# Batched 64 x 64 matmul: the first loads of b behind the first load of a, and the last casting loads one store later

## The chip, the cores and the metric

The kernel runs on one core of a Trainium2 chip. Its engines, each with its own instruction stream, are PE (matmul and weight load), DVE (vector), ACT (scalar), POOL (GpSimd) and SP (which only issues transfers here). Sixteen DMA engines move data between the HBM and the core's on-chip memory. The metric is the device time of one execution in microseconds, the median of several runs. One further execution is taken by the hardware profiler; all traces are from such executions.

## The reference

```python
def setup_inputs():
    return {
        "a": np.random.randn(1024, 64, 64).astype(np.float32),
        "b": np.random.randn(1024, 64, 64).astype(np.float32),
    }

def reference(a: np.ndarray, b: np.ndarray) -> np.ndarray:
    return np.matmul(a, b).astype(np.float32)
```

There are 1024 independent products of 64 x 64 matrices. Each of a, b and the output is 16.78 MB in float32.

## The kernel before

**Tiles.** a is worked in 8 tiles s of 128 batches, b and the output in 16 tiles t of 64 batches (`n_s` = 8, `n_t` = 16). A tile of a is 2.1 MB in HBM and becomes bf16 on its way in; a tile of b or of the output is 1.05 MB in float32.

**Loads of a** (`load_a`, L61 to L68). Four transfers per tile, one for each h, each writing 256 KB of bf16. They are issued by POOL[...]. Three buffers (`A_AHEAD` = 3).

**Loads of b** (`load_b`, L70 to L74). One transfer of 1.05 MB per tile, float32, issued on ACT for tiles 1 and 3 and on SP for the others. Four buffers (`B_AHEAD` = 4); a buffer comes free when `cast` (L111, on ACT) has made a bf16 copy of it.

**The last tile of b is different** (L112 to L115). Tile 15 isn't loaded in float32. `cast(15)` issues four transfers on POOL that write bf16 straight into `b_bf`, four rows of groups each. They wait for that buffer, which the product of tile 13 reads last.

**Compute.** `regroup(s)` (L79, DVE) reorders a tile of a; `transpose(s, w)` transposes it on PE (L88) with an identity matrix, and DVE (L94) and ACT (L96) copy the results out of PSUM; `spread(t)` (L106, DVE) lays half a tile out in blocks of 32 columns; `multiply(t)` runs 64 matmuls (L144) in four quarters, and each quarter is copied to `o_sb` by ACT (L156; in the last tile, every second quarter by DVE, L154).

**Stores** are issued by POOL, one output tile in one transfer of 1.05 MB (`put_all`, L134), the last tile in four of a quarter each (`put`, L128). A store is called one tile late (`HOLD` = 2): iteration t of the main loop issues the store of tile t - 1. There are five output buffers.

**Order.** All instructions stand in the order in which the code is written (`tc.manual_schedule()`), and each engine works its own instructions in that order. POOL's instructions, in order: the four loads of a's tile 0, a memset and an affine select that build the identity (in the helper `make_identity`), eight loads of a's tiles 1 and 2; then further loads of a mixed with the stores; at the end the stores of tiles 11 and 12, the four casting loads of tile 15, the stores of tiles 13 and 14, and the four quarter stores of tile 15. POOL's transfers form one queue. An issue on POOL also waits for the landing of the one eight places before it, since there are eight semaphores for them. SP starts with b's tiles 0 and 2, ACT with 1 and 3; neither waits for anything before its first issue but the program's start.

```python
        load_a(0)
        for t in range(B_AHEAD):
            load_b(t)
        for bd in bd_tiles:
            nc.vector.memset(bd[:], 0.0)
        make_identity(nc, identity)
        for s in range(1, A_AHEAD):
            load_a(s)
```

Of the kernel before, what the change touches and what calls it, by code (L numbers as in the profile page):

```python
# [7 lines left out]

fp32 = mybir.dt.float32
# [4 lines left out]
def kernel(  # L14
# [13 lines left out]
    nc = tc.nc  # L28
# [4 lines left out]
    n_t, n_s = B // 64, B // 128  # L33
# [6 lines left out]
    b_v = b.rearrange("(t g h) (kp u) n -> t (h kp) g (u n)", h=4, g=16, u=2)  # L40
# [16 lines left out]
    ]  # L57
    identity = consts.tile([128, 128], bf16)
    a_tiles, b_tiles, abf_tiles, at_tiles, bbf_tiles = {}, {}, {}, {}, {}
    held = {}  # L60

    def load_a(s):
        a_sb = a_pool.tile([128, 4, 16, 64], bf16, name="a_sb")
        for h in range(4):
            nc.gpsimd.dma_start(  # L65
                out=a_sb[:, h, :, :].rearrange("p v k -> p (v k)"), in_=a_v[s, h]
            )
        a_tiles[s] = a_sb  # L68

    def load_b(t):  # L70
        b_sb = b_pool.tile([128, 16, 128], fp32, name="b_sb")
        queue = nc.scalar if t in (1, 3) else nc.sync
        queue.dma_start(out=b_sb[:], in_=b_v[t])  # L73
        b_tiles[t] = b_sb  # L74

    def regroup(s):
        a_sb = a_tiles.pop(s)
        a_bf = work.tile([128, 16, 4, 64], bf16, name="a_bf")
        nc.vector.tensor_copy(a_bf[:], a_sb[:].rearrange("p h v k -> p v h k"))  # L79
        abf_tiles[s] = a_bf  # L80
        at_tiles[s] = work.tile([128, 2, 2, 128, 8], bf16, name="at_sb")

    def transpose(s, w):
        a_cols = abf_tiles[s][:].rearrange("p v h k -> p v (h k)")
        for u in range(2):
            at_ps = t_psum.tile([128, 8, 128], bf16, name="at_ps")
            for vo in range(8):
                nc.tensor.transpose(  # L88
                    at_ps[:, vo, :], a_cols[:, 2 * vo + w, u::2], identity[:]
                )  # L90
            dst = at_tiles[s][:, w, u, :, :]
            src = at_ps[:].rearrange("p vo q -> p q vo")
            if u == 0:
                nc.vector.tensor_copy(dst, src)  # L94
            else:
                nc.scalar.copy(dst, src)  # L96

    def spread(t):
        at_v = at_tiles[t // 2][:].rearrange(
            "p w u (g mp) vo -> p (w u) g (mp vo)", g=32  # L100
        )
        half = slice(16 * (t % 2), 16 * (t % 2) + 16)
        bd_v = bd_tiles[t % N_BD][:].rearrange("p (wu g) h mo -> p wu g h mo", g=16)
        for h in range(4):
            rows = slice(32 * h, 32 * h + 32)
            nc.vector.tensor_copy(bd_v[rows, :, :, h, :], at_v[rows, :, half, :])  # L106

    def cast(t):
        b_bf = work.tile([128, 16, 128], bf16, name="b_bf")
        if t < n_t - 1:  # L110
            nc.scalar.copy(b_bf[:], b_tiles.pop(t)[:])  # L111
        else:  # L112
            for gq in range(4):
                rows = slice(4 * gq, 4 * gq + 4)
                nc.gpsimd.dma_start(out=b_bf[:, rows, :], in_=b_v[t, :, rows, :])  # L115
        bbf_tiles[t] = b_bf

    def store(t):
        for piece in held.pop(t):
            piece()  # L120

    def multiply(t):
        at_bd, b_bf = bd_tiles[t % N_BD], bbf_tiles.pop(t)
        last = t == n_t - 1
        o_sb = o_pool.tile([128, 4, 4, 2, 64], fp32, name="o_sb")

        def put(gq):
            nc.gpsimd.dma_start(  # L128
                out=o_v[t, :, 4 * gq : 4 * gq + 4, :],
                in_=o_sb[:, gq, :, :, :].rearrange("p g w n -> p (g w n)"),  # L130
            )

        def put_all():
            nc.gpsimd.dma_start(  # L134
                out=o_v[t], in_=o_sb[:].rearrange("p q g w n -> p (q g w n)")
            )

        for gq in range(4):
            o_ps = o_psum.tile([128, 4, 2, 64], fp32, name="o_ps")
            for g4 in range(4):  # L140
                g = 4 * gq + g4
                for w in range(2):
                    for u in range(2):
                        nc.tensor.matmul(  # L144
                            o_ps[:, g4, w, :],
                            at_bd[:, (2 * w + u) * 16 + g, :, :].rearrange(
                                "p h mo -> p (h mo)"
                            ),
                            b_bf[:, g, 64 * u : 64 * u + 64],
                            start=(u == 0),  # L150
                            stop=(u == 1),
                        )
            if last and gq % 2:
                nc.vector.tensor_copy(o_sb[:, gq, :, :, :], o_ps[:])  # L154
            else:
                nc.scalar.copy(o_sb[:, gq, :, :, :], o_ps[:])  # L156
        held[t] = [lambda q=q: put(q) for q in range(4)] if last else [put_all]

    with tc.manual_schedule():
        load_a(0)  # L160
        for t in range(B_AHEAD):
            load_b(t)
        for bd in bd_tiles:
            nc.vector.memset(bd[:], 0.0)  # L164
        make_identity(nc, identity)
        for s in range(1, A_AHEAD):
            load_a(s)
        regroup(0)
        transpose(0, 0)
        transpose(0, 1)  # L170
        spread(0)
        cast(0)
        regroup(1)
        load_a(A_AHEAD)
        transpose(1, 0)
        for t in range(n_t):
            s, half = t // 2, t % 2
            if t + 1 < n_t:
                spread(t + 1)
            if half == 0:  # L180
                if s + 2 < n_s:
                    regroup(s + 2)
                if s + 1 + A_AHEAD < n_s:
                    load_a(s + 1 + A_AHEAD)
            multiply(t)
            if t + 1 < n_t:
                cast(t + 1)
            if t + B_AHEAD < n_t - 1:
                load_b(t + B_AHEAD)
            if half == 0 and s + 1 < n_s:  # L190
                transpose(s + 1, 1)
            if half == 1 and s + 2 < n_s:
                transpose(s + 2, 0)
            if t >= HOLD - 1:
                store(t - HOLD + 1)
        for t in range(n_t - HOLD + 1, n_t):
            store(t)

# [29 lines left out]
```

## Time and profile before

| what | value |
|---|---|
| median of 3 runs | 138.66 us (138.46 to 138.76) |
| the profiled execution | 139.03 us |
| its span, first to last instruction | 137.2 us |
| busy: PE, PEld, DVE, ACT, POOL | 59.1, 56.9, 84.5, 76.6, 45.6 us |
| HBM read, written | 33.55 MB, 16.78 MB |
| POOL's queue (a, casting loads, stores) | 25.69 MB as written, 69.9% of 16 engines' span |
| SP's and ACT's queues (b) | 13.63 and 2.10 MB, 28.4% and 4.1% |

The span is 1.8 us shorter than the execution's own time. The busy shares are averages over the whole span. A DMA share is the busy time of 16 engines; packets of different queues can overlap on one engine, so that a share in a short stretch may come out over 1. The GB/s of the profile count bytes as they are written, so a load that casts from float32 to bf16 counts with half of what it reads. "Landing" is the last semaphore update of a transfer. Times within the span are counted from the first instruction.

### The profile page before, as it was taken

The numbers are of one execution on the slowest core, as the hardware profiler recorded it, in microseconds if no ns is written. First come the engines' busy times: TensorE is split into PE (matmuls) and PEld (weight loads), VectorE is DVE, ScalarE is ACT, GpSimd is POOL, SyncE is SP. The second block draws the span as 40 slices with busy tenths as digits, with TensorE's granted clock in tenths as the row PEclk, the third lists the DMA queues.
The fourth block names the chain that finished last, engine by engine and source line by source line (L and its number), as shares of the span: only waits on it lengthen the run. The fifth ranks groups of instructions, "written<-read, shape, count | busy, mean of one in ns | idle before, by whom it ended". The sixth has DMA issues, their size and how long they took to land.

```text
span 137.2 us, 2992 instructions
## 1 busy us (share of the span) xinstructions
PE 59.1 (43%) x1280; PEld 56.9 (42%) x1280; DVE 84.5 (62%) x92; ACT 76.6 (56%) x96; POOL 45.6 (33%) x61
## 2 busy tenths in 40 slices
PE   0000072295764586450397206980085633095300
PEld 0000071295774486450396206880085633094200
DVE  5770168789799999998179903995059819501200
ACT  1030018059999999905976078840979694553100
POOL 6811242344145503351132833300213114804700
PEclk9999999559999999999559955599559995559555
DMA  2999999999999999999999999999999999999991
GB/s 72 291 304 310 303 282 260 209 256 269 237 262 274 382 295 270 318 376 374 287 269 340 377 365 274 270 364 375 382 384 379 382 382 380 382 216 315 337 289 41
DMA packets 19053, 41.61 MB, mean 303 GB/s; under 512 B 3168, under 2 KB 3168, under 8 KB 19040
## 3 DMA queue, kind: packets, MB, share of 16 engines
q0 software_dynamic: 11120, 25.69, 69.9%
q1 hardware_dynamic: 6864, 13.63, 28.4%
q10 hardware_dynamic: 1056, 2.10, 4.1%
q8 instruction: 10, 0.16, 0.5%
q14 instruction: 3, 0.02, 0.0%
HBM read 33.55 MB, written 16.78 MB: 367 GB/s over the span
## 4 chain that ended last, share of the span: by engine, by line
DMA 27%; SPq 22%; ACT 19%; issue 10%; POOL 7%; PE 6%; DVE 3%; POOLq 1%; DVEq 0%; ACTq 0%
SPq L73 22%; DMA b_sb<-in_b_dram 17%; DMA a_sb<-in_a_dram 10%; ACT o_sb L156 8%; ACT b_bf L111 6%; ACT at_sb L96 5%; PE at_ps L88 4%; POOL b_bf L115 2%; PE o_ps L144 2%; DVE a_bf L79 2%; POOL out_dram L134 2%; POOL out_dram L128 2%; DVE at_bd L106 1%; POOL a_sb L65 1%; POOLq L223 1%
## 5 line engine op out<-in xcount | busy, mean ns | idle before, releaser
L144 PE MATMUL o_ps<-b_bf,at_bd 128*128 128x64 bf16 x1024 | 41.1, 209 | 45.6 <-ACT b_bf L111 43.9
L144 PEld LDWEIGHTS <-at_bd 128*128 128x128 bf16 x1024 | 40.2, 109 | 47.5 <-issue 37.1
L106 DVE COPY at_bd<-at_sb 32x2048 bf16<-32x2048 bf16 x64 | 46.8, 731 | 21.3 <-ACT at_sb L96 20.3
L156 ACT COPY o_sb<-o_ps 128x512 f32<-128x512 f32 x62 | 33.9, 622 | 24.2 <-DMA out_dram<-o_sb 16.2
L65 POOL DMA_DIRECT2D a_sb<-in_a_dram x32 | 19.6, 617 | 39.0 <-DMA a_sb<-in_a_dram 27.2
L134 POOL DMA_DIRECT2D out_dram<-o_sb x15 | 19.2, 1278 | 38.7 <-ACT o_sb L156 21.7
L111 ACT CAST b_bf<-b_sb 128x2048 bf16<-128x2048 f32 x15 | 29.2, 1945 | 4.2 <-DMA b_sb<-in_b_dram 4.2
L88 PE MATMUL at_ps<-identity,a_bf 128*128 128x128 bf16 x256 | 20.4, 245 | 23.4 <-DVE a_bf L79 23.4
L88 PEld LDWEIGHTS <-a_bf 128*128 128x128 bf16 x256 | 18.0, 112 | 23.6 <-DVE a_bf L79 23.6
L96 ACT COPY at_sb<-at_ps 128x1024 bf16<-128x1024 bf16 x16 | 16.9, 1056 | 16.8 <-PE at_ps L88 16.8
L94 DVE COPY at_sb<-at_ps 128x1024 bf16<-128x1024 bf16 x16 | 19.5, 1222 | 4.2 <-PE at_ps L88 4.1
L79 DVE COPY a_bf<-a_sb 128x4096 bf16<-128x4096 bf16 x8 | 10.4, 1303 | 7.6 <-DMA a_sb<-in_a_dram 7.4
L164 DVE MEMSET at_bd<- 128x4096 uint32 x2 | 6.9, 3472 | 2.5 <-PEq L212 1.7
L154 DVE COPY o_sb<-o_ps 128x512 f32<-128x512 f32 x2 | 1.4, 692 | 8.8 <-PE o_ps L144 8.8
L115 POOL DMA_DIRECT2D b_bf<-in_b_dram x4 | 3.2, 806 | 4.8 <-ACT o_sb L156 4.8
L96 ACT ACT_TABLE_LOAD x1 | 1.3, 1283 | 4.4 <-issue 4.4
L128 POOL DMA_DIRECT2D out_dram<-o_sb x4 | 3.0, 754 | 1.6 <-ACT o_sb L156 0.9
L73 ACT MOVE_SHAPE b_sb<-in_b_dram x2 | 0.6, 320 | 1.7 <-issue 0.9
masks.py:199 POOL TENSOR_SCALAR_AFFINE_SELECT identity<-identity 128x128 bf16<-128x128 bf16 x1 | 0.3, 287 | 0.1
masks.py:197 POOL MEMSET identity<- 128x128 bf16 x1 | 0.3, 271 | 0.0
L212 POOL MEMSET const-float32-0.0<- 128x1 f32 x1 | 0.1, 98 | 0.2 <-issue 0.2
L212 POOL MEMSET const-bfloat16-1.0<- 128x1 bf16 x1 | 0.1, 101 | 0.0
(2 smaller groups left out, 0.2 us busy)
## 6 DMA issues: line engine op xcount, KB each, us to landing
out_dram<-o_sb POOLq DMA_DIRECT2D x15, 1024.0 KB, 21.2
a_sb<-in_a_dram POOLq DMA_DIRECT2D x32, 256.0 KB, 16.4
out_dram<-o_sb POOLq DMA_DIRECT2D x4, 256.0 KB, 7.1
b_bf<-in_b_dram POOLq DMA_DIRECT2D x4, 128.0 KB, 9.7
b_sb<-in_b_dram SPq DMA_DIRECT2D x13, 0.5 KB, 22.4
b_sb<-in_b_dram ACTq DMA_DIRECT2D x2, 0.5 KB, 18.4
```

Source lines behind the costliest of these rows:

```text
L65: nc.gpsimd.dma_start(out=a_sb[:, h, :, :].rearrange("p v k -> p (v k)"), in_=a_v[s, h])
L73: queue.dma_start(out=b_sb[:], in_=b_v[t])
L79: nc.vector.tensor_copy(a_bf[:], a_sb[:].rearrange("p h v k -> p v h k"))
L88: nc.tensor.transpose(at_ps[:, vo, :], a_cols[:, 2 * vo + w, u::2], identity[:])
L94: nc.vector.tensor_copy(dst, src)
L96: nc.scalar.copy(dst, src)
L106: nc.vector.tensor_copy(bd_v[rows, :, :, h, :], at_v[rows, :, half, :])
L111: nc.scalar.copy(b_bf[:], b_tiles.pop(t)[:])
L134: nc.gpsimd.dma_start(out=o_v[t], in_=o_sb[:].rearrange("p q g w n -> p (q g w n)"))
L144: nc.tensor.matmul(o_ps[:, g4, w, :], at_bd[:, (2 * w + u) * 16 + g, :, :].rearrange("p h mo -> p (h mo)"), b_bf[:, g, 64 * u : 64 * u + 6 ...
L156: nc.scalar.copy(o_sb[:, gq, :, :, :], o_ps[:])
L164: nc.vector.memset(bd[:], 0.0)
```

## The change

Two places are edited, and the imported helper that built the identity is written out.

First, the memset of the identity tile moves to POOL's stream between the first and the second load of a's tile 0, and the loads of b's tiles 0 (on SP) and 1 (on ACT) get a dependence on that memset. As an engine works in order, the memset comes after POOL has issued the first load of a. The affine select stays where it was, behind the four loads of tile 0.

Second, in the iteration t = 14 of the main loop, `cast(15)` comes after `store(13)` instead of ahead of it. POOL's order at the end becomes: stores of tiles 11, 12 and 13, the four casting loads, the store of tile 14, the four quarter stores. No other engine's order changes.

```diff
@@ -57,11 +56,13 @@
-    held = {}
+    held, begun = {}, []
 
     def load_a(s):
         a_sb = a_pool.tile([128, 4, 16, 64], bf16, name="a_sb")
         for h in range(4):
+            if s == 0 and h == 1:
+                begun.append(nc.gpsimd.memset(identity[:], 0.0))
             nc.gpsimd.dma_start(
                 out=a_sb[:, h, :, :].rearrange("p v k -> p (v k)"), in_=a_v[s, h]
             )
@@ -70,7 +71,16 @@
         queue = nc.scalar if t in (1, 3) else nc.sync
-        queue.dma_start(out=b_sb[:], in_=b_v[t])
+        load = queue.dma_start(out=b_sb[:], in_=b_v[t])
+        if t < 2:
+            tc.add_manual_dep(
+                load.ins,
+                begun[0].ins.name,
+                mybir.DependencyInfo(
+                    mybir.DependencyClass.Sync, mybir.DependencyReason.DATA
+                ),
+                reason="first load of a goes ahead",
+            )
         b_tiles[t] = b_sb
@@ -162,7 +172,15 @@
-        make_identity(nc, identity)
+        nc.gpsimd.affine_select(
+            out=identity[:],
+            in_=identity[:],
+            compare_op=mybir.AluOpType.not_equal,
+            fill=1.0,
+            base=0,
+            pattern=[[-1, 128]],
+            channel_multiplier=1,
+        )
@@ -183,7 +201,7 @@
             multiply(t)
-            if t + 1 < n_t:
+            if t + 1 < n_t - 1:
                 cast(t + 1)
@@ -193,6 +211,8 @@
             if t >= HOLD - 1:
                 store(t - HOLD + 1)
+            if t == n_t - 2:
+                cast(t + 1)
```

More of the change, by code (lines that the diff above doesn't have):

```diff
@@ L5 @@
 from concourse import bass_utils, mybir
-from concourse.masks import make_identity
 from concourse._compat import with_exitstack
```

## The prediction

> **What bounds the kernel now.** I read the 40 slices first, then the queues and landings, then the chain of waits, then the stretches at both ends, because the change touches the first 4 us and the last 23 us.
>
> ```profile
> DMA  2999999999999999999999999999999999999991
> DMA packets 19053, 41.61 MB, mean 303 GB/s; under 512 B 3168, under 2 KB 3168, under 8 KB 19040
> ...
> SPq L73 22%; DMA b_sb<-in_b_dram 17%; DMA a_sb<-in_a_dram 10%; ACT o_sb L156 8%; ACT b_bf L111 6%; ACT at_sb L96 5%; PE at_ps L88 4%; POOL b_bf L115 2%; PE o_ps L144 2%; DVE a_bf L79 2%; POOL out_dram L134 2%; POOL out_dram L128 2%; DVE at_bd L106 1%; POOL a_sb L65 1%; POOLq L223 1%
> ```
>
> The DMA row is the bound: 38 of 40 slices show the 16 engines busy for 90% or more, while DVE, the busiest compute engine, has 62%. The chain of waits names a's first tile, ACT work and then SP's queue. I give that chain less weight: it follows who released whom, but if the engines always have other bytes to move, a wait that goes only changes the order of the bytes. The time is then first byte, plus bytes at the rate their mix allows, plus the drain.
>
> The stretches at the start, in time order (columns: length, busy time of PE, PEld, DVE, ACT, POOL, clock, DMA share, GB/s counted as written):
>
> ```profile
> 1.00:2.00 1.00, 0.00 (x0) 0.00 (x0) 0.33 (x1) 0.32 (x1) 0.71 (x2) 1.00 0.00 0
> 2.00:3.00 1.00, 0.00 (x0) 0.00 (x0) 1.00 (x1) 0.30 (x1) 1.00 (x2) 1.00 0.52 139
> 3.00:4.00 1.00, 0.00 (x0) 0.00 (x0) 1.00 (x1) 0.00 (x0) 0.93 (x4) 1.00 0.90 215
> 4.00:5.00 1.00, 0.00 (x0) 0.00 (x0) 1.00 (x1) 0.00 (x0) 1.00 (x3) 1.00 1.01 352
> 5.00:6.00 1.00, 0.00 (x0) 0.00 (x0) 0.20 (x2) 0.00 (x0) 1.00 (x3) 1.00 1.08 291
> ```
>
> The first bytes move after 2 us and the rate climbs for 2 us. The timeline says whose they can be:
>
> ```profile
> 0.79 0.86 ACTq L73 DMA_DIRECT2D b_sb<-in_b_dram  x1
> 0.80 24.16 SPq L73 DMA_DIRECT2D b_sb<-in_b_dram  x3
> 1.29 2.32 POOL L65 DMA_DIRECT2D a_sb<-in_a_dram  x4 [0.84 <-POOLq L212]
> ...
> 16.77 1.23 DVE L79 COPY a_bf<-a_sb 128x4096 bf16<-128x4096 bf16 x1 [7.36 <-DMA a_sb<-in_a_dram]
> ```
>
> b's loads are issued 0.5 us ahead of a's. In the packet records b0 has its first packet at 2.39 us, a0 its first at 4.93 and b1, issued on ACT at 0.79, at 5.18: SP's load has the engines alone for 2.5 us. From there on a and b share, and a0 is complete at 16.65.
>
> The end:
>
> ```profile
> 114.97 3.20 POOL L115 DMA_DIRECT2D b_bf<-in_b_dram  x4 [4.77 <-ACT o_sb L156]
> 118.16 1.27 POOL L134 DMA_DIRECT2D out_dram<-o_sb  x1
> 124.32 1.16 POOL L134 DMA_DIRECT2D out_dram<-o_sb  x1 [4.89 <-ACT o_sb L156]
> 124.82 3.30 PE L144 MATMUL o_ps<-b_bf,at_bd 128*128 128x64 bf16 x64 [1.42 <-DMA b_bf<-in_b_dram]
> 129.39 0.75 POOL L128 DMA_DIRECT2D out_dram<-o_sb  x1 [0.55 <-DVE o_sb L154]
> ...
> 118.00:120.00 2.00, 0.15 (x4) 0.15 (x4) 0.66 (x1) 1.79 (x1) 1.43 (x2) 0.50 1.03 385
> 122.00:124.00 2.00, 1.40 (x27) 1.26 (x24) 0.00 (x0) 1.48 (x3) 0.00 (x0) 0.69 1.60 184
> 128.00:130.00 2.00, 0.12 (x3) 0.00 (x0) 0.69 (x1) 0.00 (x0) 1.36 (x2) 0.50 1.02 326
> 131.00:132.00 1.00, 0.00 (x0) 0.00 (x0) 0.00 (x0) 0.00 (x0) 0.00 (x0) 0.50 1.02 291
> 134.00:135.00 1.00, 0.00 (x0) 0.00 (x0) 0.00 (x0) 0.00 (x0) 0.00 (x0) 0.50 0.22 86
> ```
>
> POOL's queue works in order: stores 11 and 12, the four casting loads of tile 15, store 13, store 14, four quarter stores of tile 15. The casting loads land at 124.69, 125.53, 126.32 and 127.04, store 13 at 129.82, store 14 at 132.72, the quarters at 133.66 to 135.77. The last quarter is issued 2.35 us after the last casting load lands (129.39 - 127.04) and lands 6.38 us after its issue, because it stands behind a backlog. Stores alone run at 385 GB/s at 118 us and at 291 at 131 us; the casting loads fill the engines at only 184 (122 to 124).
>
> **What the Trainium skill says.** "DMA: Bandwidth & Descriptors", section "Queues, rings and completion order": each engine round-robins between its queues, a packet at a time. From 5 us on the trace agrees (a and b share); in the first 2.5 us it doesn't, since b1 and a0 had been issued and got nothing.[...] The same page, "Latency and other measured facts", gives about 0.6 us to the first byte for a load from SP or ACT and about 1 us for one from GpSimd. Here SP's took 1.59 us (0.80 to 2.39), longer; GpSimd's alone on idle engines is in no part of this trace. "Anatomy of one DMA" says that most of some 2 us fixed cost is the wait for the write's receipt; the trace has 0.43 us from the last packet's end (135.34) to the last landing (135.77).
>
> **The change part by part.**
>
> Part 1, the start. The memset moves between a0's first and second issue. POOL's first issue ends at 1.98; with 0.27 for the memset (its own row) the marker is set at about 2.25, and the first b loads on SP and ACT go at about 2.3 instead of 0.8, so 1.5 us later. Behind them on the same queues stand b2 (SP, at 2.06 before), b3 (ACT, at 2.33, its issue lasting 4.32 us) and ACT's table load at 6.68. All shift by some 1.5 us. b2 and b3 would land by about 20 and 25.5 and are cast after 36; the table is first used at 19.98: covered. a0's other three issues shift by 0.27 us, but chunk 0 keeps the queue busy for longer; the affine select is wanted by the first transpose only. The explicit memset and select replace the helper's same two instructions: nothing.
>
> What isn't covered is the engines' idle time. From the windows, before moved 139 + 215 + 352 + 291 = 997 KB as written by 6.0 us; 83 KB of that are a's, by the packet records, and each is two bytes read, which makes about 1,080 KB of HBM traffic. With the gate, b's first packet is at about 2.3 + 1.59 = 3.9, and a's is unknown: not before 1.98 + 0.6 = 2.6, not after 4.93 as now. At the early end a alone at about 400 GB/s (a and b together carry 400 to 404 from 6 us on) moves 1,360 KB by 6.0, a gain of 280 KB or 0.7 us. At the late end, b alone from 3.9 with before's climb (some 510 KB in its first 2.1 us) and a as now (166 KB) move some 680 KB, a loss of 1.0 us. I take the middle, about 3.5 us: 2.5 us at an average of 395 give 990 KB, a loss of 90 KB, **+0.2 us**.
>
> a0 comes earlier: with up to 2.5 us of the engines to itself it may land near 12 to 14 instead of 16.65. Compute and b4's load (which waits for the first cast, now 22.3 to 24.2) then start earlier too. I cost that at nothing: between 18.2 and 28.3 SP's queue is without a packet, but a's own chunks keep the engines full. What is late next is the DMA engines.
>
> Part 2, the end. Store 13 goes ahead of the casting loads. It waits for the copies of tile 13 (done at 115.02), so it issues at about 115.1 (1.27 us), and the loads at 116.3 to 119.5 instead of 114.97 to 118.17: covered, as the queue reaches them after 120 only. Nobody else waits behind POOL until store 14 at 124.3. In the queue a store of 256 packets at 174 ns over 16 engines takes 2.8 us, so the casting loads land 2.8 us later, the last at 129.8, and the last quarter issues at 132.2 instead of 129.4. The bytes after that are unchanged. Whether this costs depends on the least time from issue to landing: 0.75 for the issue, 0.6 to 2.5 for the first packet, 0.8 for four packets per engine at about 200 ns, 0.43 to the landing, so 2.6 to 4.5 us. It then lands at 134.8 to 136.7 where the backlog allows 135.77: 0 to +0.9; I take 3.8 us, so 136.0: **+0.25 us**. Below zero: with store 13 moved away, the final run of stores is 2 MB instead of 3 MB. If the slow 291 GB/s comes from that run's length, 1.05 MB at 385 instead of 291 saves 0.9 us, capped at 0.7 by the latency.
>
> Sum: 139.03 (span 137.2 and 1.83 around it) + 0.2 + 0.25 = 139.48 on the profiled execution; that one was 0.37 above the median, so **139.1** for the median. A difference of 0.2% is 0.28 us, about what a measurement here can tell.
>
> **Rivals.**
> - Start gains. a's stream reaches idle engines before 3.0 us and runs at full rate at once, where b climbed slowly: -0.5 at the start (from 2.8 us at 400 GB/s: 1,280 KB against 1,080), tail hidden: 138.66 - 0.5, 138.1 to 138.2. For: from 2.39 to 4.0 us b moved 354 KB, where 400 GB/s would give 640. Against: cold first packets could slow a in the same way. It decides from a first a packet at about 3.0 us on downwards.
> - Tail gains. The write run after the casting loads is shorter and faster, -0.7, with +0.2 at the start: 138.2. For: 385 against 291 GB/s. Against: the 2 MB moved ahead may become slow instead.
> - All hidden. The same bytes, the same full engines, a0 and b0 swap places: 138.7.
> - Both exposed. a doesn't start before 4.5 us (+1.0), and the last quarter has the long latency (+0.7): 140.3. For: today's 4.93.
> - The change doing nothing at the start (b issued late but a not ahead) falls under the last.
>
> **How the numbers follow.** Forecast 0.38, start gains 0.18, tail gains 0.18, all hidden 0.14, both exposed 0.12. The forecast's own range is 138.9 to 139.7, and a little of it (0.02) lies within 0.2%. Faster 0.36, same 0.16, slower 0.48. The range 137.8 to 140.3 takes in both gains with 0.3 us to spare and reaches to the exposed case.
>
> **What would show it.** A first a packet at 2.6 to 4 us and DMA GB/s near 0 from 2 to 3; a0's regroup on DVE well before 16.77; the first cast on ACT earlier, though the end doesn't follow. At the end store 13 issued ahead of the casting loads, these landing 2 to 3 us later, a last quarter issued near 132 and landing in 4 us or less, and DMA share below 1 before it. I am wrong if the span falls by over 0.3 us, in particular if the earlier compute carries through to the end: then the DMA engines weren't the bound that I read.

## The result, and the profile after

The changed kernel takes 142.71 us, median of six runs (141.57 to 143.48), against 138.51 us (138.29 to 138.76) for the kernel before: a ratio of 1.0293, 95% interval 1.0233 to 1.0353. A second set of six runs gave 141.96 us against 138.53, ratio 1.0246 (1.0215 to 1.0277). It is slower by 3.4 to 4.2 us, where 0.45 us was forecast. The profiled execution took 141.57 us, 2.54 us more than the one before (139.03); the fastest run of its set was profiled, so the traces show less of the loss than the medians.

The page of the changed kernel: the span, the DMA and GB/s rows of the 40 slices, and the shares of the chain of waits.

```profile
span 139.8 us, 2992 instructions
...
DMA  2999999999999999999999999999999999999973
GB/s 19 189 307 306 305 307 304 298 271 250 230 273 268 373 304 269 318 372 375 284 271 342 381 355 274 274 373 379 383 383 372 387 382 382 318 260 155 287 217 109
...
DMA 56%; issue 27%; POOL 13%; POOLq 1%
DMA a_sb<-in_a_dram 38%; DMA out_dram<-o_sb 17%; POOL out_dram L144 6%; POOL a_sb L66 3%; POOL b_bf L125 2%; POOL out_dram L138 2%; POOLq L243 1%; POOL identity L175 0%; POOL identity L65 0%; POOLq L144 0%; POOLq L175 0%; POOLq L138 0%; POOLq L125 0%; POOLq L66 0%; POOLq L232 0%
```

In the first two slices 19 and 189 GB/s stand where 72 and 291 stood, but these count bytes as written, and up to 6.4 us all of them are a's, of which twice as many are read. The last six slices have 318, 260, 155, 287, 217 and 109. SP's queue, 22% of the chain before, is gone from it: the chain now runs along POOL's own queue (a's loads 38%, the stores 17%).

The stretches at the start (columns: length; busy time of PE, PEld, DVE, ACT, POOL; clock; DMA share; GB/s as written), and one instruction of the timeline:

```profile
2.00:3.00 1.00, 0.00 (x0) 0.00 (x0) 1.00 (x1) 0.02 (x1) 1.00 (x3) 1.00 0.49 33
3.00:4.00 1.00, 0.00 (x0) 0.00 (x0) 1.00 (x1) 0.62 (x1) 0.95 (x3) 1.00 0.77 86
4.00:5.00 1.00, 0.00 (x0) 0.00 (x0) 1.00 (x1) 0.00 (x0) 1.00 (x3) 1.00 1.09 201
5.00:6.00 1.00, 0.00 (x0) 0.00 (x0) 0.20 (x2) 0.00 (x0) 1.00 (x3) 1.00 1.12 199
```

```profile
12.97 1.23 DVE L89 COPY a_bf<-a_sb 128x4096 bf16<-128x4096 bf16 x1 [3.56 <-DMA a_sb<-in_a_dram]
```

a goes ahead as it was meant to: its first packet is at 2.66 us (4.93 before), and tile 0 is regrouped at 12.97 instead of 16.77. b's tile 0, issued at 2.28, has its first packet at 6.44: now b waits behind a, as a did behind b. By 6.0 us the engines have moved 33 + 86 + 201 + 199 = 519 KB as written, 1,038 KB read. In the profile of before they have moved 1,098 KB (the prediction counted 83 KB of a's there; its packet records have 49 packets of 2,048 B, 100 KB). That profile is the lowest of six runs with the old opening, which have 1,098 to 1,264 KB, 1,186 in the mean; the four runs with both gates have 1,036 to 1,075, 1,052 in the mean. At 400 GB/s the start costs 0.15 us in bytes by the two profiles and 0.3 us by the means.

The end, as timeline (start, length, engine, line, operation) and as stretches:

```profile
115.49 1.23 POOL L144 DMA_DIRECT2D out_dram<-o_sb  x1 [3.42 <-ACT o_sb L166]
...
116.70 3.20 POOL L125 DMA_DIRECT2D b_bf<-in_b_dram  x4
...
130.36 3.57 PE L154 MATMUL o_ps<-b_bf,at_bd 128*128 128x64 bf16 x64 [8.39 <-DMA b_bf<-in_b_dram]
...
134.95 0.75 POOL L138 DMA_DIRECT2D out_dram<-o_sb  x1 [0.21 <-issue]
```

```profile
118.00:120.00 2.00, 1.36 (x31) 1.36 (x31) 1.57 (x2) 1.15 (x2) 1.90 (x3) 0.74 1.04 365
122.00:124.00 2.00, 0.00 (x0) 0.00 (x0) 0.00 (x0) 0.59 (x1) 1.11 (x1) 0.91 1.01 287
126.00:128.00 2.00, 0.00 (x0) 0.00 (x0) 0.00 (x0) 0.00 (x0) 0.00 (x0) 0.50 1.24 134
132.00:134.00 2.00, 1.93 (x37) 1.77 (x34) 0.72 (x2) 0.59 (x1) 1.53 (x3) 0.50 0.50 170
136.00:138.00 2.00, 0.00 (x0) 0.00 (x0) 0.00 (x0) 0.00 (x0) 0.00 (x0) 0.50 0.78 229
```

PE sits idle for 8.39 us before the last tile, waiting for a casting load (1.42 before). The casting loads land at 130.22 to 132.43 instead of 124.69 to 127.04, 5.4 us later, and the last quarter store is issued at 134.95 and lands at 138.39, 3.44 us after its issue: there is no backlog ahead of it any more. From 132 to 134 the DMA share is 0.50: on average half of the engines have no work while the last product is made. Stores alone fall from 365 to 287 GB/s between 118 and 124. From 124 on the casting loads are in the count, with half of what they read: 134 GB/s from 126 to 128, against 184 in the like stretch before (122 to 124).

One more reading of the traces carries what follows. The Trainium skill, "DMA: Bandwidth & Descriptors", section "Why a DMA increments its semaphore by 16 and not by 1", says that each of the 16 engines adds one to a transfer's semaphore when its own share has landed. The traces agree: POOL's transfers have 16 updates each. The time between the first and the last of them is how far the engines are out of step, called the spread here. For the fourth and last chunk of a's tile 0 it is 0.53 us before and 2.16 us after. It doesn't stay at that: by the store of tile 9, at about 112 us, the two kernels have 2.31 and 3.11 us. With 16 updates, the ninth stands here for the middle engine.

### The profile page after: what moved, and what is told of

Same layout as the page of the kernel before. It is cut to its first block, busy times and chain, and to the rows that moved or that the text cites. A ratio compares the mean times of both kernels' runs of the same rounds, so it can differ in the third digit from the quotient of the medians.

```text
span 139.8 us, 2992 instructions
## 1 busy us (share of the span) xinstructions
PE 62.0 (44%) x1280; PEld 59.7 (43%) x1280; DVE 85.3 (61%) x92; ACT 77.1 (55%) x96; POOL 46.4 (33%) x61
## 3 DMA queue, kind: packets, MB, share of 16 engines
q1 hardware_dynamic: 6864, 13.63, 27.6%
## 4 chain that ended last, share of the span: by engine, by line
DMA 56%; issue 27%; POOL 13%; POOLq 1%
DMA a_sb<-in_a_dram 38%; DMA out_dram<-o_sb 17%; POOL out_dram L144 6%; POOL a_sb L66 3%; POOL b_bf L125 2%; POOL out_dram L138 2%; POOLq L243 1%; POOL identity L175 0%; POOL identity L65 0%; POOLq L144 0%; POOLq L175 0%; POOLq L138 0%; POOLq L125 0%; POOLq L66 0%; POOLq L232 0%
## 5 line engine op out<-in xcount | busy, mean ns | idle before, releaser
L154 PE MATMUL o_ps<-b_bf,at_bd 128*128 128x64 bf16 x1024 | 42.5, 213 | 50.3 <-ACT b_bf L121 36.4
L154 PEld LDWEIGHTS <-at_bd 128*128 128x128 bf16 x1024 | 41.7, 112 | 52.1 <-issue 41.0
L116 DVE COPY at_bd<-at_sb 32x2048 bf16<-32x2048 bf16 x64 | 47.6, 744 | 19.6 <-ACT at_sb L106 18.6
L66 POOL DMA_DIRECT2D a_sb<-in_a_dram x32 | 20.1, 641 | 39.9 <-DMA a_sb<-in_a_dram 29.2
L98 PE MATMUL at_ps<-identity,a_bf 128*128 128x128 bf16 x256 | 21.9, 255 | 21.7 <-DVE a_bf L89 21.7
L98 PEld LDWEIGHTS <-a_bf 128*128 128x128 bf16 x256 | 19.3, 118 | 22.0 <-DVE a_bf L89 22.0
```

The source lines that it names most:

```text
L66: nc.gpsimd.dma_start(out=a_sb[:, h, :, :].rearrange("p v k -> p (v k)"), in_=a_v[s, h])
L98: nc.tensor.transpose(at_ps[:, vo, :], a_cols[:, 2 * vo + w, u::2], identity[:])
L154: nc.tensor.matmul(o_ps[:, g4, w, :], at_bd[:, (2 * w + u) * 16 + g, :, :].rearrange("p h mo -> p (h mo)"), b_bf[:, g, 64 * u : 64 * u + 6 ...
```

## The experiments

Ratios are to the kernel before in the same batch (medians of 138.24 to 138.56 us), with 95% intervals. Spreads and landings, in us, are from each run's one profile.

| run | median us | ratio (95%) | spread, a's 4th chunk | spread, store of tile 9 | last casting load | last landing |
|---|---|---|---|---|---|---|
| before | 138.51 | | 0.53 | 2.31 | 127.04 | 135.77 |
| after | 142.71 | 1.0293 (1.0233 to 1.0353) | 2.16 | 3.11 | 132.43 | 138.39 |
| after_again | 141.96 | 1.0246 (1.0215 to 1.0277) | 2.15 | 3.12 | 133.16 | 139.13 |
| gate_only | 140.91 | 1.0175 (1.0149 to 1.0201) | 3.07 | 4.62 | 128.15 | 137.76 |
| cast_only | 139.34 | 1.0059 (1.0038 to 1.0080) | 0.67 | 2.85 | 130.55 | 136.33 |
| gate_b0 | 138.98 | 1.0030 (1.0017 to 1.0044) | 1.02 | 2.46 | 127.75 | 136.00 |
| gate_b1 | 138.95 | 1.0022 (1.0008 to 1.0037) | 1.10 | 2.72 | 127.58 | 135.84 |
| late_all | 139.74 | 1.0073 (1.0044 to 1.0101) | 0.70 | 2.70 | 128.35 | 136.73 |
| after_reads | 144.20 | 1.0422 (1.0402 to 1.0443) | 1.90 | 3.42 | 135.45 | 141.22 |
| deep_b | 144.91 | 1.0465 (1.0440 to 1.0489) | 0.99 | 4.11 | 133.36 | 141.60 |
| b3 | 141.27 | 1.0202 (1.0165 to 1.0238) | 0.57 | 1.84 | 126.69 | 138.27 |
| store13_sp | 139.27 | 1.0070 (1.0058 to 1.0083) | 0.65 | 2.66 | 130.42 | 135.96 |
| store1314_sp | 139.49 | 1.0091 (1.0077 to 1.0106) | 0.77 | 2.73 | 131.19 | 136.21 |

### Each half alone

`gate_only` is the changed kernel with the old order at the end:

```diff
-            if t + 1 < n_t - 1:
+            if t + 1 < n_t:
                 cast(t + 1)
...
-            if t == n_t - 2:
-                cast(t + 1)
```

> Only the first half of the change: the gate on the first two b loads, the casting loads ahead of store 13 as before. Theory S (the prediction's start term was right, the loss is all at the end): +0.1 to +0.4 us on the median of before, so 138.6 to 138.9. Theory R (the earlier end of b's loads, 116.6 against 117.8, is what lengthens the run of pure stores and slows the end): +1 us or more.

`cast_only` is the kernel before with the new order at the end, that is, with these lines the other way round.

> Only the second half: store 13 ahead of the casting loads, no gate. Theory S: the whole loss but 0.2 us is here, so +2.4 to +4.5 us, 141 to 143, with the last casting load landing 4 us or more later than the 127.04 of before and under 4 us from the last quarter's issue to its landing. Theory R: under +2 us, since b ends at its old time.

The gate alone costs 1.75% (2.4 us), the casting loads' place 0.59% (0.8 us). Theory S is refuted: most of the loss is in the half that it priced at 0.2 us. The two add up to 2.34%, within the intervals of both measurements of the whole change (2.33 to 3.53 and 2.15 to 2.77). Theory R, which put the loss on b's earlier end, was right on both numbers, but this doesn't make its mechanism the cause: in gate_only b ends at 117.10, only 0.72 us before the 117.82 of before, and gate_b1, below, ends b earlier still (116.87) and costs 0.3 us.

The end of before, and then of gate_only, in the same columns (the line of before from 134 to 135 us has a share of 0.22):

```profile
133.00:134.00 1.00, 0.00 (x0) 0.00 (x0) 0.00 (x0) 0.00 (x0) 0.00 (x0) 0.50 0.73 250
...
135.00:136.00 1.00, 0.00 (x0) 0.00 (x0) 0.00 (x0) 0.00 (x0) 0.00 (x0) 0.50 0.01 4
```

```profile
133.00:134.00 1.00, 0.00 (x0) 0.00 (x0) 0.00 (x0) 0.00 (x0) 0.00 (x0) 0.50 0.90 279
134.00:135.00 1.00, 0.00 (x0) 0.00 (x0) 0.00 (x0) 0.00 (x0) 0.00 (x0) 0.50 0.38 148
135.00:136.00 1.00, 0.00 (x0) 0.00 (x0) 0.00 (x0) 0.00 (x0) 0.00 (x0) 0.50 0.12 45
136.00:137.00 1.00, 0.00 (x0) 0.00 (x0) 0.00 (x0) 0.00 (x0) 0.00 (x0) 0.50 0.07 25
```

A DMA share of 0.07 is one engine of sixteen (0.0625). From 136 us on a single engine works off its part of the last stores, with 15 done. In the last store's 16 updates the ninth comes at 134.65 (134.53 before) and the last at 137.76 (135.77 before). The middle engine is 0.12 us later than before, the last one 1.99 us. As a pool the engines lost almost nothing; one of them is late, and the kernel waits for it.

That this is the lag of the start, carried along, the trace doesn't show. The engines of before get out of step too, only later: their spread is 0.5 us up to 28 us, 1.7 at 35.6, and 2.2 to 2.5 from 41 to 113 us. In gate_only it falls from 3.1 to 2.1 us by 37 us, rises to 4.9 at 46, and is 4.6 for store 9. At store 12 (last update 124.02) the last engine is only 1.25 us behind the middle one, where before has 1.44. The straggler of the end comes up after that: from the last casting load to store 13 the last update takes 4.41 us (128.15 to 132.56) and the ninth 2.74 (125.72 to 128.46). In that stretch the packet records have one packet of the queue that the page calls q8 instruction, 16 KB from 130.48 to 131.51. before has one as well (128.58 to 129.61), without such a step. Whether the slowest engine served it isn't shown, so this packet stays an untested rival for a part of the 1.99 us.

In cast_only the engines stay in step at the start (0.67 us) and the end is the one that the prediction described, a little larger:

```profile
122.00:124.00 2.00, 0.82 (x19) 0.70 (x16) 0.00 (x0) 1.17 (x2) 0.25 (x1) 0.87 1.05 278
...
130.00:132.00 2.00, 2.00 (x38) 1.84 (x35) 0.69 (x1) 0.66 (x2) 1.45 (x2) 0.50 0.56 196
```

Stores alone slow to 278 GB/s ahead of the casting loads, and while the last product is made (130 to 132) the share is 0.56. The last casting load lands at 130.55, 3.51 us later than before. The last quarter store follows it by 2.48 us (issue at 133.03) and lands 3.30 us after that.

### Which part of the gate costs

`gate_b0` and `gate_b1` gate one of the two loads only (`if t == 0:` and `if t == 1:` in place of `if t < 2:`; base: gate_only). `late_all` keeps both gates but puts b ahead of a again, everything later:

```diff
-            if s == 0 and h == 1:
-                begun.append(nc.gpsimd.memset(identity[:], 0.0))
+            if s == 0 and h == 0:
+                for i in range(6):
+                    begun.append(nc.gpsimd.memset(identity[:], 0.0))
...
-                begun[0].ins.name,
+                begun[3].ins.name,
```

> The gate on b's tile 0 (SP) alone; tile 1 on ACT is free, the end as before. Theory J (the cost of the gate is that a long stream of b joins DMA engines that a already keeps busy, which puts the 16 engines out of step and leaves one of them to finish last): b's tile 1 now runs ahead of a, a joins it, so the four landings of a's tile 0 stay within 1 us between first and last engine for most chunks, and the time is 138.3 to 139.3. Theory G (it costs what it costs because SP's first load is late): as with the whole gate, 140.5 or more.

> The gate on b's tile 1 (ACT) alone; tile 0 on SP is free, the end as before. Theories J and G: no cost, 138.1 to 138.7, since tile 1 had no packet before 5.18 us anyway. Theory P (any late join of a queue costs, also ACT's): 139 or more.

> Six memsets on POOL ahead of a's first load, b's first two loads gated on the fourth of them: all first loads are about 1.5 us later and b is ahead of a as in the kernel before. Theory J: the engines stay in step (landings of a's tile 0 within 0.8 us between the engines) and the time grows by the shift alone, +1.2 to +1.7 us, with the last engine finishing 1 to 1.5 us after the middle one as before. Theory G (waiting on POOL for the first b loads is itself what puts the engines out of step): +3 us or more.

gate_b0 costs 0.30%, gate_b1 0.22%, both gates together 1.75%. So neither load's lateness is the cost: while one b load still runs ahead of a, the other can be late for 0.3 to 0.4 us. Theory G is refuted by gate_b0, and in its other form by late_all. gate_b1 came out above its expected range, by a little, so a late second queue isn't quite free (spread 1.10 against 0.53).

late_all has both gates too, and holds b's loads until 1.82 us (gate_only 2.29) and a's first until 2.19 (1.30), yet it costs 0.73% (1.0 us), less than gate_only and a little less than expected. Its first b packet is at 3.41 us, 1.0 us later than before, and a's at 4.96, the old order, and the spread is 0.70. Its end:

```profile
134.00:135.00 1.00, 0.00 (x0) 0.00 (x0) 0.00 (x0) 0.00 (x0) 0.00 (x0) 0.50 0.69 242
135.00:136.00 1.00, 0.00 (x0) 0.00 (x0) 0.00 (x0) 0.00 (x0) 0.00 (x0) 0.50 0.19 74
136.00:137.00 1.00, 0.00 (x0) 0.00 (x0) 0.00 (x0) 0.00 (x0) 0.00 (x0) 0.50 0.01 4
```

The drain has the shape of before, 1 us later (0.73, 0.22, 0.01 from 133 on there). The middle engine ends at 135.27 and the last at 136.73: a shift of the whole, no straggler. All four runs with both gates have a spread of 1.90 to 3.07 us in a's fourth chunk; the nine in which a load of b runs ahead of a have 0.53 to 1.10. So it is the order, a alone on the engines when both b queues come in, that puts the engines out of step in the first 14 us, and the same order costs 2.4 us where a single late load costs 0.3 or 0.4 and the late start in the old order 1.0. Why an engine falls back in that order isn't shown: the records don't say which engine a packet ran on. In gate_only the spread is 0.63 us for a's first chunk, 1.41 for the second, and 3.07 for the fourth, that is, it grows between 5 and 14 us, while b's queues (first packets 5.83 and 6.91) come in.

### Stores without loads beside them

`stores_only` leaves everything out but 16 full stores from five tiles of zeros. `after_reads` adds two loads of b behind tile 14's, to tiles that nobody reads:

```diff
                 load_b(t + B_AHEAD)
+                if t + B_AHEAD == n_t - 2:
+                    for i in range(2):
+                        more = consts.tile([128, 16, 128], fp32, name=f"more{i}")
+                        nc.sync.dma_start(out=more[:], in_=b_v[i])
```

> Leaves out all loads and all arithmetic: five tiles of zeros are stored to the 16 output tiles on the same queue. Theory W (a run of stores without loads beside it slows down after about 3 us): about 380 GB/s in the first 3 us of traffic, 260 to 310 afterwards, the 16.78 MB in about 55 to 60 us. Theory E (the slow rate belongs to the end of this program, to the mix of queued transfers or to the tile's work beside it): 370 to 385 GB/s throughout, about 44 us.

> The changed kernel with two more loads on SP behind b's tile 14, 2.1 MB of b read again into tiles that nobody uses; the output is unaffected. Theory W: while these reads run, from about 116 to 130 us, all traffic together is near 380 GB/s where the changed kernel had 300 or less from 119.5 to 125, so the added bytes (5.5 us at 380 GB/s) cost 3 us at most. Theory E: the rate stays near 300 or less in that stretch and the time grows by 5 us or more.

stores_only, in stretches (only DVE and POOL have instructions, so the columns are length, their busy times, clock, DMA share, GB/s):

```profile
10.00:20.00 10.00, 1.56 (x1) 7.00 (x7) 1.00 1.00 266
...
62.00:66.00 4.00, 0.00 (x0) 0.00 (x0) 1.00 0.66 221
66.00:70.00 4.00, 0.00 (x0) 0.00 (x0) 1.00 0.46 175
```

With every engine busy (share 1.00) stores alone run at 266 GB/s, not 385, so theory W holds for the rate. It missed two things: there is no fast start (267 from 6 to 10 us already), and the engines don't share the work's time evenly. In the last store's 16 updates eight come at 63.5 to 64.0 us and eight at 69.5 to 70.9, so that the single run took 73.67 us, not 55 to 60. Stores alone put the engines out of step as well: the spread is 1.0 us for the first store and grows with each of the next eleven, to 9.4.

after_reads while its extra reads run:

```profile
118.00:120.00 2.00, 2.00 (x40) 2.00 (x40) 1.96 (x4) 0.76 (x2) 2.00 (x3) 0.50 1.02 378
122.00:124.00 2.00, 0.00 (x0) 0.00 (x0) 0.00 (x0) 0.00 (x0) 1.17 (x1) 1.00 1.03 384
126.00:128.00 2.00, 0.00 (x0) 0.00 (x0) 0.00 (x0) 0.00 (x0) 0.00 (x0) 0.50 1.01 379
```

From 122 to 124 the engines move 384 GB/s where the changed kernel moved 287. The 2.1 MB cost 1.5 us against the changed kernel's first set (144.20 and 142.71) and 2.2 us against its second (141.96), not the 5.5 us that they take at 380 GB/s. Loads beside the stores come at less than half of their price there, as theory W says.

### More and fewer buffers for b

`deep_b` is the kernel before with `B_AHEAD = 6`, `b3` with `B_AHEAD = 3`, nothing else.

> The kernel before with six buffers for b instead of four, no gate and the old order at the end, so that SP's queue need not pause at 18 us and join again at 28. Theory J: the spread of a's landings between the engines, which grows from 0.7 to 1.7 us at that join, stays under 1 us until the next pause, and the time falls by 0.3 to 1.5 us. Theory S (the end alone decides): within 0.3 us of before.

> The kernel before with three buffers for b instead of four. Theory W (stores alone are slow, loads beside them keep the engines fast): b's last load ends at 121 to 126 us instead of 117.8, the stretch at 290 to 300 GB/s before the end shrinks, and the time falls by 0.3 to 1.5 us. Theory S (only the order at the very end counts): within 0.3 us of before, or slower if compute now waits for b.

Both were expected to be faster and both are slower. deep_b has b's last load landed at 105.68 instead of 117.82, 12 us earlier, and then:

```profile
104.00:106.00 2.00, 0.00 (x0) 0.00 (x0) 0.00 (x0) 2.00 (x3) 1.15 (x1) 0.50 1.01 379
108.00:110.00 2.00, 2.00 (x37) 2.00 (x35) 1.69 (x3) 1.47 (x3) 0.00 (x0) 0.50 1.02 315
116.00:118.00 2.00, 1.26 (x44) 1.26 (x44) 0.36 (x1) 2.00 (x4) 0.55 (x1) 1.00 0.99 276
```

Full engines, 276 GB/s: stores run alone from b's last landing to the first packet of the casting loads at 123.37, for 17.7 us. deep_b costs 6.35 us (144.91 less 138.56), about half a microsecond for each that b ends earlier. By that slope the 0.72 us of gate_only are worth an estimated 0.4 of its 2.4 us, and that is what is left of theory R; gate_b1, with b ended 0.95 us earlier, paid 0.3 us in all.

The spread didn't do what theory J expected either. SP's queue doesn't pause in deep_b, but the spread rises from 0.96 to 1.73 us between the landings at 35.52 and 38.29, as it rises in before from 0.69 to 1.71 between 32.52 and 35.62. So that step comes without the pause and the join at 28 us too. In both profiles the first 16 KB packet of q8 instruction, which takes 0.97 us, falls into it (from 35.50 and from 33.20); in gate_only the spread doesn't rise across that packet (33.07). Whether these packets drive the engines apart isn't tested here.

b3 failed for another reason. SP's queue has no packet from 17.58 to 37.44 us, and later compute waits for b:

```profile
POOL out_dram L134 <- ACT o_sb L156: 48.9, 11, 8.3
...
ACT b_bf L111 <- DMA b_sb<-in_b_dram: 20.2, 8, 5.5
```

(Waits: who for whom, total us, times, longest.) These two were 21.7 and 4.2 us before. b ends at 119.94, short of the expected 121 to 126, and the stores still come last. Of three, four and six buffers four are the fastest, between these two losses; five weren't tried.

### A second profile, and store 13 on another queue

`after_again` is the changed kernel without an edit. `store13_sp` and `store1314_sp` are the kernel before with this (and `t in (13, 14)`):

```diff
-            nc.gpsimd.dma_start(
+            queue = nc.sync if t == 13 else nc.gpsimd
+            queue.dma_start(
```

> The changed kernel once more, for a second profile, since its first one (141.57 us) was the fastest of six runs and three of them took 143.3 to 143.5. Theory J + latency: the last casting load lands where the slowest engine puts it, and the end follows 5.7 to 6.1 us later; an execution of 143 us or more shows that load at 133.5 us or later and a spread between the engines of over 2.2 us in the fourth landing of a. If instead the longer execution has the same landing of the casting loads (132 to 133), the extra time lies behind it, and the theory lacks a part.

> The kernel before with store 13 issued on SP, whose queue is empty by then, instead of POOL. The casting loads keep their place right behind store 12 and share the engines with store 13 instead of standing ahead of it or behind it. Theory W (loads and stores side by side keep the engines fast): from 118 to 128 us the traffic is near 370 GB/s instead of 300 to 330, the last casting load lands at 127 to 130, and the time falls by 0.3 to 1.3 us. Theory S (only the place of the casting loads counts): within 0.3 us of before, or slower as their landing moves out.

> Stores 13 and 14 both on SP; the quarter stores of tile 15 then follow the casting loads on POOL's queue and share the engines with store 14. Theory W: as with store 13 alone or up to 0.5 us better, since no quarter waits behind store 14. Theory S: within 0.3 us of before, or slower.

No run of the second set reached 143 us, so what made three runs of the first take 143.3 to 143.5 wasn't seen in a profile and stays open. The two profiles that there are differ as the latency says: casting load 0.73 us later, end 0.74 us later, and 5.97 us between the two events against 5.96. Their spread in a's fourth chunk is the same (2.15 and 2.16), so that part of the expectation missed; the second one's engines drift further during store 13 (spread 4.74 against 2.94), in the slow stretch of stores.

The attempts at a faster kernel failed: +0.70% and +0.91%. Store 13 and the casting loads did run side by side, but slowly:

```profile
124.00:126.00 2.00, 0.04 (x2) 0.07 (x3) 0.00 (x0) 0.00 (x0) 1.17 (x1) 0.50 1.38 214
```

```profile
q1 hardware_dynamic: 8928, 14.68, 31.9%
```

(store13_sp: a stretch, and SP's queue with packets, MB and share.) The queue has 2,064 packets more than before (6,864) for 1.05 MB, so SP issues the store in packets of some 512 B, where POOL's queue has it in 256 of 4,096 B. Beside these the casting loads land up to 1.9 us apart (0.7 to 0.9 before), the last at 130.42, so what theory W expected here, 370 GB/s, missed: a load beside a store isn't fast in every form. No version tried here beats the kernel before.

## Why the prediction was wrong

- **The bound.** That the DMA engines are the bound held, and so did the remark on the chain of waits: compute began 3.8 us earlier (12.97 against 16.77) and the end didn't follow.
- **Start, bytes: the size right, partly by luck.** +0.2 us was forecast; the bytes by 6 us are short by 0.15 us in the two profiles and by 0.3 us in the means. But a's first packet, forecast for about 3.5, came at 2.66, and b's, forecast for 3.9, at 6.44. What a's early start won, its slow climb (33 and 86 GB/s as written from 2 to 4 us, so 66 and 172 read) and b's lateness took back. The early bound of 2.6 us used for POOL's load the 0.6 us that the prediction quotes for SP and ACT; a's load took 1.38 us from the start of its issue (1.28 to 2.66).
- **Start, order: the step that failed.** The prediction cost "a0 comes earlier" at nothing, because "a's own chunks keep the engines full". It treated 16 engines as one pool that is slow only when it lacks bytes. With both gates in place that step has a price: 2.4 us in place of 0.2, of which an estimated 0.4 at most is b's earlier end. The engines were full, but not in step: with a alone in front, the slowest engine is 1.9 to 3.1 us behind the first by the fourth chunk, and a transfer lands with its slowest engine. At the end of gate_only the middle engine is 0.12 us later than before and the last one 1.99. late_all shows that late loads in the old order cost a mere 1.0 us. How the loss gets from the first 14 us to the end stays open: on the way the last engine of gate_only was once no further behind than that of before.
- **End, the place of the casting loads: right in mechanism, one term too small.** The chain "casting load, product, copy, issue, landing" sets the end, as described. Of its terms, the delay of the casting loads was 3.51 us in cast_only where 2.8 was taken, though store 13's own landing follows store 12's by 2.73 us (123.29, 126.02): the casting loads behind it then took 4.53 us to the last landing, and 3.60 behind store 12 before. In the changed kernel both are long: 4.15 us (123.73, 127.88) and 4.55. The issue followed after 2.48 (2.35 taken), the landing after 3.30 (3.8 taken). Sum: 136.33 against a forecast 136.0, +0.56 in the profile where +0.25 was forecast; +0.8 in the median.
- **Together.** In the changed kernel the last casting load lands 1.88 us later than in cast_only (132.43 and 130.55), and the end is 2.06 us later. That is not one late engine: the ninth of this load's updates is 1.92 us later as well (130.16 and 128.24), the spread at store 9 differs by 0.26 us only, and the last store's 16 updates lie within 0.45 us. By the packet records all engines together have read and written 0.27 MB less than in cast_only by 116 us and 0.58 MB less by 130, an estimated 0.7 and 1.5 us at 380 GB/s. So half of the difference comes up while stores are alone, and in the casting loads behind them; that stretch begins 0.76 us earlier here (b ends at 116.61 and 117.37). Why the engines fall behind as a pool isn't shown.
- **Rivals.** "Start gains" had its condition met, a first packet before 3.0 us, and still lost: a climbed slowly, as its own counter-argument said, and no bytes were won. "Tail gains" fell to its own counter-argument: the 2 MB of stores moved ahead became slow (365 to 287 GB/s from 118 to 124). "Both exposed" named the right side with the wrong reasons: a did start early, and the latency was short (3.44 us). No rival put a price on the order of the streams or on engines that differ among themselves, and the range ended at 140.3.

## What to carry to other kernels

Where a kernel is bound by DMA, an order of first loads isn't free because the bytes are the same: look at the 16 updates of a transfer's semaphore, at several places and not at the start alone, and at whether the DMA share at the end falls in one step or thins out to one engine. Keep loads beside stores for as long as compute doesn't wait for them: here, after some 3 us, stores alone ran at 260 to 315 GB/s, and with a load stream beside them at 380, so finishing the loads earlier made the kernel slower. A transfer that the last product waits for should be priced by its slowest engine's landing plus the whole chain behind it, and put where a backlog covers that chain (8.7 us of stores behind it before, 5.96 us of bare chain after).

## What was not expected of the hardware

- 16 stores of 1.05 MB with nothing beside them took 266 GB/s with all engines busy, and half of the engines finished about 6 us before the others (their last updates are at 63.5 to 64.0 and at 69.5 to 70.9 us).
- After mixed traffic a run of stores alone keeps 380 GB/s for about 3 us and then falls below 320 (in deep_b 379 at 104 to 106 us, 315 at 108 to 110), while stores on an idle chip don't show that fast phase.
- With a streaming, b's two queues wait 4.2 and 4.6 us from issue to first packet (2.28 to 6.44 and 2.27 to 6.83); with b streaming a waits 3.6 us (1.29 to 4.93).
- The 16 DMA engines don't stay in step in any run: in before the spread is 0.5 us up to 28 us and 2.2 to 2.5 from 41 to 113 us.
- The same store is cut into 256 packets of 4,096 B when POOL issues it and into some 2,060 of 512 B when SP does.
